# Operands of the input projection and of stick-breaking attention kept in DRAM in two parts, and half of the weights' rests formed in PSUM

## The chip, the cores and the metric

The kernel runs on one core of one Trainium2 chip. The metric is the device time of one execution in microseconds. PE is TensorE, DVE VectorE, ACT ScalarE, POOL GpSimd; SP is the queue that issues most DMAs.

## The reference, cut to what matters

The reference is one layer of a decoder trunk in float32: 2048 tokens, width 1024. One projection feeds four groups of heads; their outputs are normed, projected and followed by an MLP.

```python
h = rms_norm(x, norm1_w[l])
cols = split_cols(h @ w_in[l], IN_SIZES)
...
s_q, s_k, s_v = cols[14:17]
...
y_d = stick_breaking_mixer(s_q.reshape(B, S, SB_HEADS, HEAD_DIM), s_k.reshape(B, S, SB_HEADS, HEAD_DIM),
                           s_v.reshape(B, S, SB_HEADS, HEAD_DIM))
```

The group of heads that the change touches is the last one, with 4 heads of 64 columns:

```python
def stick_breaking_mixer(q, k, v):
...
        z = jnp.einsum('bqhd,bkhd->bhqk', q_blk, k).astype(f32) * scale
        strict = kpos[None, :] < (t0 + jnp.arange(Q_BLOCK))[:, None]
        log_1m = jnp.where(strict, jax.nn.log_sigmoid(-z), 0.0)
        rem = lax.cumsum(log_1m, axis=3, reverse=True) - log_1m
        a = jnp.where(strict, jnp.exp(jax.nn.log_sigmoid(z) + rem), 0.0)
        return jnp.einsum('bhqk,bkhd->bqhd', a.astype(v.dtype), v)
```

## The kernel before, in words

Products of two float32 matrices are made of float32r products: an operand is split in a high part (a copy rounded to float32r) and a low part, the rest (operand minus high part), and three products high·high, high·low and low·high are summed in PSUM. `split_s` (L212) does the split: ACT copies the high part, another engine, mostly DVE, subtracts.

The program has three phases: `front`, the attention phase (`attention.main`) and `tail` (output projection and MLP). The change lies in `front` and in `stick`, which `front` runs in its last part.

**The projection.** The transposed, normed input is held for half of the tokens at a time (`hth`, `htl`). The weight columns are cut in ten chunks ("nq", "m", "nk", "sv" with tokens on the partitions, 0 to 5 with columns on the partitions; 2540 columns in all). For each chunk and each half of the tokens an object of the class `Weights` (L367) loads eight row blocks of the weights (`wraw`, L378) and splits each (`wh`, `wl`, L386, scaled by the norm's weight). So every block of the weights is loaded and split twice, once per half. `ch_mm` and `tok_mm` make the products, 24 per output tile. `channel` (L614) and `sb_v` (L608) store the columns of the stick-breaking q, k and v to DRAM (`sbqd`, `sbkd`, `sbvd`), unsplit. In the second half the chunks "nk", 3, 4 and 5 are held back: they are the filling work of `others()`.

**Stick-breaking attention.** `stick` (L1196) goes through 4 heads and 4 blocks of 512 queries each (16 units); `ahead` loads a unit's q, k and v as `srq`, `srk`, `srv` and splits them (`qq` and `sql`, `kk`, `svp`). For each unit and each of its key blocks `weights` makes, per 128 queries, the logits (PE to `pmm`), two sigmoids on ACT (`bt`, `sg`), a scan on DVE that multiplies up the products from the right (`ce`, L1256) and a product on POOL (`sg`, L1258). One step later `values` transposes the weights 128 keys at a time (PE, L1297, to `ptr`), splits the 128x512 result (`ah` by ACT, `al` by DVE, L1301), and `product` multiplies both parts with the values (`svp`, to `pacc`). There are 160 such splits: 112 of 512 columns and 16 each of 384, 256 and 128.

**What sets the order.** The last loop of `front` pairs the steps of `stick` with steps of `others()` at a fixed rate (150 filling steps on 388 steps of `stick`), each filling step being placed behind the last product issued. Beyond that the framework's scheduler orders the instructions of each engine. The first part of the attention phase's preparation (`nx.early()`) also runs as filling work.

## Time and profile before

| | |
|---|---|
| median of 3 runs | 3097.89 us (3091.86 to 3104.19) |
| the profiled execution | 3101.34 us, of which the span of its instructions is 3099.6 us |
| mean granted clock of TensorE | 0.970 |
| projection, first half of the tokens | 0 to about 333 us |
| projection, second half, without the chunks held back | about 333 to 509 us |
| `stick` with its filling work | about 509 to 905 us |
| attention phase, then the tail | from 905 us to the end |

The profile gives busy time per engine; a view by stretches gives the busy time in each stage, the granted clock of PE (1 is 2.4 GHz, one half is 1.2 GHz) and the share of the DMA engines. The time before an engine's instruction in which it stood idle is put down to whatever released that instruction last.

### The profile page before, as it was taken

The numbers are of one execution on the slowest core, as the hardware profiler recorded it, in microseconds if no ns is written. First come the engines' busy times: TensorE is split into PE (matmuls) and PEld (weight loads), VectorE is DVE, ScalarE is ACT, GpSimd is POOL, SyncE is SP. The second block draws the span as 40 slices with busy tenths as digits, with TensorE's granted clock in tenths as the row PEclk, the third lists the DMA queues.
The fourth block names the chain that finished last, engine by engine and source line by source line (L and its number), as shares of the span: only waits on it lengthen the run. The fifth ranks groups of instructions, "written<-read, shape, count | busy, mean of one in ns | idle before, by whom it ended". The sixth has DMA issues, their size and how long they took to land. (4 is left out here: it accounts for less than half of the span.)

```text
span 3099.6 us, 43934 instructions
## 1 busy us (share of the span) xinstructions
PE 2921.3 (94%) x14123; PEld 2327.5 (75%) x14123; DVE 2301.5 (74%) x4894; ACT 1693.7 (55%) x3440; POOL 1353.4 (44%) x1311
## 2 busy tenths in 40 slices
PE   7999999899888999998989989999999999989999
PEld 7868888677755666666768778787888778877887
DVE  7844478998877686777668777657444599999999
ACT  5622455777775778786765444456555533324331
POOL 1300012444655666765622257735222244364434
PEclk9999999899988999999999999999999999999999
DMA  6343434211320110010034468936333544365432
GB/s 162 100 113 86 128 97 110 61 53 45 84 84 23 28 33 22 29 42 15 9 114 143 170 212 299 314 107 203 110 109 109 211 163 156 122 206 172 150 131 73
DMA packets 283977, 356.49 MB, mean 115 GB/s; under 512 B 74207, under 2 KB 185483, under 8 KB 283491
## 3 DMA queue, kind: packets, MB, share of 16 engines
q1 hardware_dynamic: 251859, 310.03, 32.1%
q10 hardware_dynamic: 31344, 41.82, 3.6%
q0 software_dynamic: 544, 1.84, 0.2%
q8 instruction: 112, 1.84, 0.2%
q14 instruction: 118, 0.97, 0.1%
HBM read 248.04 MB, written 105.59 MB: 114 GB/s over the span
## 5 line engine op out<-in xcount | busy, mean ns | idle before, releaser
L931 POOL TENSOR_TENSOR pw<-pf,ph 128x512 fp32r<-128x512 f32 (+2 forms) x264 | 325.9, 1243 | 170.0 <-ACT pf L930 120.8
L138 PE MATMUL ptr<-form,big 128*128 128x512 f32 x1152 | 280.4, 392 | 7.8 <-ACT ft L1857 4.2
L138 PE MATMUL pmm<-form,big 128*128 128x512 f32 x1152 | 278.5, 391 | 0.9 <-ACT big L216 0.9
L925 ACT ACTIVATE ph<-pmm 128x512 fp32r<-128x512 f32 (+2 forms) x366 | 210.7, 576 | 102.0 <-PE pmm L138 67.7
L138 PEld LDWEIGHTS ptr<-form,big 128*128 128x128 f32 x1152 | 216.3, 188 | 56.9 <-ACT ft L1857 5.1
L138 PEld LDWEIGHTS pmm<-form,big 128*128 128x128 f32 x1152 | 216.1, 188 | 48.1 <-ACT big L216 1.3
L1258 POOL TENSOR_TENSOR sg<-sg,ce 128x512 f32<-128x512 f32 (+3 forms) x160 | 161.3, 1009 | 178.6 <-DVE ce L1256 130.8
L138 PE MATMUL pmm<-big 128*128 128x512 f32 (+5 forms) x816 | 217.2, 394 | 4.7 <-DVE accp L2054 2.4
L216 ACT ACTIVATE big<-raw 128x1024 fp32r<-128x1024 f32 (+2 forms) x116 | 100.9, 883 | 183.7 <-PE ptr L138 106.4
L138 PE MATMUL pmm<-big,big 128*128 128x512 f32 (+5 forms) x672 | 178.1, 392 | 12.2 <-DVE accp L2054 10.0
L138 PE MATMUL pmm<-big,ar 128*128 128x512 f32 x736 | 185.1, 401 | 1.9 <-DVE ar L217 1.9
L138 PEld LDWEIGHTS pmm<-big 128*128 128x128 f32 (+2 forms) x816 | 154.4, 193 | 40.8 <-ACT op L216 5.2
L217 DVE TENSOR_TENSOR big<-hr,big 128x512 fp32r<-128x512 f32 (+1 forms) x125 | 136.8, 1096 | 60.2 <-ACT big L216 60.1
L138 PE MATMUL ptr<-big 128*128 128x512 f32 (+3 forms) x639 | 174.8, 396 | 4.5 <-DVE mx L1153 2.1
L217 DVE TENSOR_TENSOR big<-yr,big 128x512 fp32r<-128x512 f32 (+1 forms) x125 | 130.7, 1048 | 53.9 <-ACT big L216 53.5
L138 PEld LDWEIGHTS pmm<-big,ar 128*128 128x128 f32 x736 | 138.2, 191 | 32.4 <-DVE ar L217 2.4
L2054 DVE TENSOR_TENSOR accp<-accp,ptr 128x512 f32<-128x512 f32 x224 | 151.8, 678 | 13.0 <-PE ptr L138 12.6
L2054 DVE TENSOR_TENSOR accp<-accp,pmm 128x512 f32<-128x512 f32 x224 | 151.7, 677 | 9.7 <-PE pmm L138 9.7
L138 PEld LDWEIGHTS pmm<-big,big 128*128 128x128 f32 (+2 forms) x672 | 125.0, 189 | 43.2 <-DVE accp L2054 10.9
L138 PE MATMUL ptr<-big,big 128*128 128x512 f32 (+3 forms) x512 | 144.4, 402 | 8.3 <-DVE accp L2054 3.7
L930 ACT ACTIVATE pf<-pmm 128x512 f32<-128x512 f32 (+2 forms) x264 | 152.2, 577 | 0.0
L138 PEld LDWEIGHTS ptr<-big 128*128 128x128 f32 (+1 forms) x639 | 121.7, 191 | 36.0 <-DVE mx L1153 3.8
(504 smaller groups left out, 8384.2 us busy)
## 6 DMA issues: line engine op xcount, KB each, us to landing
ud<-ft ACTq DMA_DIRECT2D x124, 256.0 KB, 2.0
xt<-x SPq DMA_DIRECT2D x32, 512.0 KB, 3.5
yr<-ffn_w SPq DMA_DIRECT2D x16, 1024.0 KB, 5.1
hr<-ffn_w SPq DMA_DIRECT2D x16, 1024.0 KB, 5.9
rawb<-ffn_w SPq DMA_DIRECT2D x28, 512.0 KB, 6.8
wsd<-rawb SPq DMA_DIRECT2D x28, 512.0 KB
rawb<-ud SPq DMA_DIRECT2D x28, 512.0 KB, 4.3
raw<-wsd SPq DMA_DIRECT2D x28, 512.0 KB, 3.5
```

What stands on the lines that cost most here:

```text
L138: anchor[0] = pe.matmul(o, l, r, start=start, stop=stop)
L216: act.activation(hi, src, AF.Copy)
L217: (eng or dve).tensor_tensor(lo, src, hi.bitcast(F32), ALU.subtract)
L925: act.activation(ph[:, 0:n], pl[:, 0:n], AF.Exp)
L930: act.activation(pf[:, 0:n], pl[:, 0:n], AF.Exp)
L931: sub.tensor_tensor(pw[:, 0:n], pf[:, 0:n], ph[:, 0:n].bitcast(F32), ALU.subtract)
L1258: pool.tensor_tensor(sg[:, o:512], sg[:, o:512], ce[:, o + 1:513], ALU.mult)
L2054: dve.tensor_tensor(acc[p][:, t], acc[p][:, t], pt, ALU.add)
```

## The change

It does three things.

1. The first half stores each split block of weights (both parts, one tile `whl`) to DRAM arrays `kept`, three blocks behind the split; the second half loads the two parts from there and splits nothing.
2. The stick-breaking q, k and v are split where they leave PSUM, and both parts are stored; `ahead` only loads the parts to where they are used.
3. In `values`, for every second 128 keys, the transposed weights stay in PSUM as an open sum. ACT copies the high part, PE adds the product of that part with minus the identity, so the low part is left in PSUM, and ACT copies that. The other splits stay.

```diff
+            def store_weights(left):
+                while len(stores) > left:
+                    o, w = stores.pop(0)
+                    sync.dma_start(o, w)
...
                 def load(self, k):
                     while len(self.ws) <= k:
                         n = self.n
                         c = len(self.ws)
+                        whl = wp.tile([P, 2, CW], F32R, name="whl", tag="whl", bufs=NWT)
+                        wh, wl = whl[:, 0], whl[:, 1]
+                        self.ws.append((wh, wl))
+                        if not self.first:
+                            sync.dma_start(whl[:, :, :n].bitcast(F32), self.kept[c])
+                            continue
...
-                        wh = wp.tile([P, CW], F32R, name="wh", tag="wh", bufs=12)
-                        wl = wp.tile([P, CW], F32R, name="wl", tag="wl", bufs=12)
                         split_s(raw[:, :n], wh[:, :n], wl[:, :n], n1w[:, c:c + 1],
                                 heng=pool if self.raw is not None and c % 2 else None)
-                        self.ws.append((wh, wl))
+                        stores.append((self.kept[c], whl[:, :, :n].bitcast(F32)))
+                        store_weights(3)
...
+            def sb_v(i, pt):
+                vt = op.tile([P, H, 2, HD], F32R, name="vhl", tag="cout")
+                split_s(pt[:, 0:256].rearrange("p (h d) -> p h d", h=H), vt[:, :, 0], vt[:, :, 1])
+                sync.dma_start(sbvd[i * P:(i + 1) * P].rearrange("p h c -> p (h c)"),
+                               vt.rearrange("p h s d -> p (h s d)").bitcast(F32))
...
-                    if kind in ("q", "k", "kv"):
+                    if kind in ("q", "k"):
+                        hl = [op.tile([P, 512], F32R, name="chl%d" % n, tag="cout") for n in range(2)]
+                        split_s(pt, *hl)
+                        for o, t in zip(sbqd if kind == "q" else sbkd, hl):
+                            sync.dma_start(o[ct * P:(ct + 1) * P, t0:t0 + 512], t.bitcast(F32))
...
+        minus = kp.tile([P, P], F32R, name="minus")
+        act.activation(minus, ident, AF.Copy, scale=-1.0)
...
-                sync.dma_start(rk[g * 64:(g + 1) * 64, :], sbkd[hs, tsl])
-                sync.dma_start(rq[g * 64:(g + 1) * 64, :], sbqd[hs, tsl])
-            sync.dma_start(rv, sbvd[tsl, hs].rearrange("(i p) d -> p i d", p=P))
-            yield
-            act.activation(kk, rk, AF.Copy)
-            dve.tensor_tensor(kk[64:128], rk[64:128], kk[64:128].bitcast(F32), ALU.subtract)
-            yield
-            act.activation(qq, rq, AF.Copy)
-            dve.tensor_tensor(ql[0:64], rq[0:64], qq[0:64].bitcast(F32), ALU.subtract)
-            yield
-            split_s(rv, vp[:, :, 0:64], vp[:, :, 64:128])
-            yield
+                sync.dma_start(kk[g * 64:(g + 1) * 64, :].bitcast(F32), sbkd[g][hs, tsl])
+                sync.dma_start(qq[g * 64:(g + 1) * 64, :].bitcast(F32), sbqd[0][hs, tsl])
+            sync.dma_start(ql[0:64].bitcast(F32), sbqd[1][hs, tsl])
+            sync.dma_start(vp.bitcast(F32), sbvd[tsl, h].rearrange("(i p) d -> p i d", p=P))
+            for _ in range(4):
+                yield
...
-                    pe.transpose(pt[:, t * P:(t + 1) * P], sgs[t][:, o + jj * P:o + (jj + 1) * P], ident)
+                    pe.matmul(pt[:, t * P:(t + 1) * P], sgs[t][:, o + jj * P:o + (jj + 1) * P], ident,
+                              start=t == f, stop=False, is_transpose=True, skip_group_check=True)
...
-                split_s(pt[:, f * P:], ah[:, f * P:], al[:, f * P:])
+                if jj % 2:
+
+                    act.activation(ah[:, f * P:], pt[:, f * P:], AF.Copy)
+                    if flight:
+                        product()
+                    pe.matmul(pt[:, f * P:], minus, ah[:, f * P:], start=False, stop=True, skip_group_check=True)
+                    act.activation(al[:, f * P:], pt[:, f * P:], AF.Copy)
+                else:
+                    split_s(pt[:, f * P:], ah[:, f * P:], al[:, f * P:])
```

How the scheduler then orders the work is shown at three places. The first is DVE about halfway through `stick`, at the end of a unit's last key block and the start of the next: `ce` are scans, `al` the low parts of transposed weights. Before:

```order
L1256 SCALAR_TENSOR_TENSOR ce_9967<-bt_9966,pmm_9968 128x512
L217 TENSOR_TENSOR al_9871<-ptr_9865,ah_9870 128x512
L217 TENSOR_TENSOR al_9908<-ptr_9902,ah_9907 128x512
L217 TENSOR_TENSOR al_9934<-ptr_9928,ah_9933 128x512
L1256 SCALAR_TENSOR_TENSOR ce_9990<-bt_9989,ce_9878,pmm_9991 128x512
L1256 SCALAR_TENSOR_TENSOR ce_10022<-bt_10021,ce_9915,pmm_10023 128x512
L1256 SCALAR_TENSOR_TENSOR ce_10047<-bt_10046,ce_9941,pmm_10048 128x512
L217 TENSOR_TENSOR al_9957<-ptr_9951,ah_9956 128x512
```

The same place now:

```order
L1275 SCALAR_TENSOR_TENSOR ce_9673<-bt_9672,pmm_9674 128x512
L218 TENSOR_TENSOR al_9577<-ptr_9571,ah_9576 128x512
L218 TENSOR_TENSOR al_9639<-ptr_9633,ah_9638 128x512
L1275 SCALAR_TENSOR_TENSOR ce_9696<-bt_9695,ce_9584,pmm_9697 128x512
L1275 SCALAR_TENSOR_TENSOR ce_9727<-bt_9726,ce_9620,pmm_9728 128x512
L1275 SCALAR_TENSOR_TENSOR ce_9752<-bt_9751,ce_9646,pmm_9753 128x512
L218 TENSOR_TENSOR al_9689<-ptr_9683,ah_9688 128x512
```

Of four subtractions between the scans two are left; the scans stand as they did.

The second place is the same stretch on PE. `cp,sg` are the transposes, `minus` the new product, `pacc1` the products with the values, `kk,qq` and `kk,sql` the logits. Before, eight transposes are followed by logits and by the products of earlier parts:

```order
L1297 MATMUL ptr_9928<-cp_63,sg_9764 128x128
L1297 MATMUL ptr_9928<-cp_63,sg_9793 128x128
L1297 MATMUL ptr_9928<-cp_63,sg_9823 128x128
L1297 MATMUL ptr_9928<-cp_63,sg_9850 128x128
L138 MATMUL pmm_10023<-kk_9529,qq_9661 128x512
L138 MATMUL pmm_10023<-kk_9529,sql0_7012 128x512
L138 MATMUL pmm_10048<-kk_9529,qq_9661 128x512
L138 MATMUL pmm_10048<-kk_9529,sql0_7012 128x512
L138 MATMUL pacc1_9790<-ah_9870,svp_9053 128x512
L138 MATMUL pacc1_9790<-al_9871,svp_9053 128x512
```

Now:

```order
L1316 MATMUL ptr_9606<-cp_63,sg_9530 128x128
L1316 MATMUL ptr_9606<-cp_63,sg_9556 128x128
L1325 MATMUL ptr_9542<-ah_9544,minus_6840 128x128
L139 MATMUL pacc1_9495<-ah_9544,svp_9249 128x256
L139 MATMUL pmm_9753<-kk_9247,qq_9368 128x512
L139 MATMUL pmm_9753<-kk_9247,sql0_6842 128x512
L1325 MATMUL ptr_9606<-ah_9611,minus_6840 128x512
L139 MATMUL pacc1_9495<-al_9545,svp_9249 128x256
```

And ACT's copies around the same product, now:

```order
L217 ACTIVATE ah_9576<-ptr_9571 128x512
L1322 ACTIVATE ah_9611<-ptr_9606 128x512
L1326 ACTIVATE al_9545<-ptr_9542 128x128
L1272 ACTIVATE bt_9751<-pmm_9753 128x512
L1326 ACTIVATE al_9612<-ptr_9606 128x512
```

On PE four other products stand between the last transpose into this bank (`ptr_9606`) and the product with minus the identity; over the 80 of them the count goes from 2 to 28 (two of the 80 have under 4, half have 14 or more). On ACT the copy of the low part stands mostly 3 to 8 instructions behind that of the high part. Behind the last transpose of `stick` PE's order is the same, row for row, as before.

The third place is SP at the start of the program. Before:

```order
L422 DMA xt<-x 128x1024 x3
L464 DMA gq<-mla_q_norm 96x1
L465 DMA gq<-mla_k_norm 96x1
L564 DMA ngn<-nsa_q_norm 64x1
L565 DMA ngn<-nsa_k_norm 64x1
L564 DMA ngn<-nsa_q_norm 64x1
```

Now:

```order
L436 DMA xt<-x 128x1024 x3
L487 DMA gq<-mla_q_norm 96x1
L488 DMA gq<-mla_k_norm 96x1
L587 DMA ngn<-nsa_q_norm 64x1
L588 DMA ngn<-nsa_k_norm 64x1
L370 DMA kept_nq<-whl 256x1x256 x5
```

Five stores of split weights now stand ahead of the fifth load of x. Over the whole program SP issues 1244 DMAs where it issued 1172: 120 loads of `w_in` fewer, 80 stores to and 80 loads from `kept` more, 16 more stores of q and k, and 16 more loads in `ahead`.

## Rows read from the trace of the kernel before

**Rows 1.** The page: busy time, share of the span and instructions of each engine.

```profile
PE 2921.3 (94%) x14123; PEld 2327.5 (75%) x14123; DVE 2301.5 (74%) x4894; ACT 1693.7 (55%) x3440; POOL 1353.4 (44%) x1311
```

**Rows 2.** Busy time by stretches: engines, granted clock, DMA share, GB/s.

```profile
0.00:333.00 333.00, 307.20 (x1730) 262.11 (x1731) 200.32 (x799) 144.75 (x334) 61.31 (x91) 0.97 0.44 114
333.00:509.00 176.00, 172.31 (x1067) 153.59 (x1066) 110.02 (x432) 87.91 (x232) 23.90 (x73) 1.00 0.42 113
509.00:905.00 396.00, 345.07 (x1881) 276.29 (x1880) 364.93 (x657) 287.93 (x653) 196.45 (x373) 0.93 0.26 70
1100.00:1300.00 200.00, 187.73 (x925) 134.19 (x926) 149.02 (x417) 153.13 (x350) 133.09 (x131) 0.96 0.10 29
2200.00:2600.00 400.00, 392.55 (x1696) 318.88 (x1695) 255.93 (x330) 189.88 (x276) 128.93 (x73) 0.99 0.42 146
```

**Rows 3.** Waits of PE, 509 to 905 us: total us, times, longest us.

```profile
PE pmm L138 <- DVE ce L1256: 24.4, 28, 4.7
PE pacc L138 <- DVE al L217: 7.0, 11, 1.6
PE pmm L138 <- DVE rky L199: 4.0, 3, 3.0
PE pmm L138 <- DVE rkt L198: 3.5, 3, 2.9
```

**Rows 4.** Groups of DVE, 509 to 905 us: busy us, mean ns, idle before.

```profile
L1256 DVE TENSOR_TENSOR_SCAN ce<-bt,ce,pmm 128x512 f32<-128x512 f32 x96 | 119.5, 1266 | 4.8 <-ACT sg L1254 4.2 <-POOL ce L1251 0.3 <-issue 0.3
L217 DVE TENSOR_TENSOR al<-ptr,ah 128x512 fp32r<-128x512 f32 (+3 forms) x160 | 92.1, 595 | 3.9 <-ACT ah L216 3.5
L1256 DVE TENSOR_TENSOR_SCAN ce<-bt,pmm 128x128 f32<-128x128 f32 (+1 forms) x64 | 50.4, 806 | 2.9 <-ACT sg L1254 0.8 <-issue 0.7 <-POOL al L1303 0.5
L223 DVE SCALAR_TENSOR_TENSOR wl<-wraw,n1w,wh 128x256 fp32r<-128x256 f32 (+2 forms) x28 | 18.3, 668 | 1.0 <-ACT wh L220 0.9
L1224 DVE TENSOR_TENSOR kk<-srk,kk 64x512 fp32r<-64x512 f32 x16 | 13.0, 815 | 1.0 <-ACT kk L1223 0.4
L1227 DVE TENSOR_TENSOR sql<-srq,qq 64x512 fp32r<-64x512 f32 x16 | 12.1, 755 | 0.5 <-PE ptr L1297 0.4
L217 DVE TENSOR_TENSOR svp<-srv,svp 128x256 fp32r<-128x256 f32 x16 | 8.8, 549 | 3.4 <-ACT svp L216 3.3
```

**Rows 5.** Groups of ACT, 509 to 905 us.

```profile
L216 ACT ACTIVATE ah<-ptr 128x512 fp32r<-128x512 f32 (+3 forms) x160 | 84.7, 548 | 48.3 <-PE ptr L1297 38.6 <-DVE ce L1256 3.7 <-issue 2.6
...
L220 ACT ACTIVATE wh<-wraw,n1w 128x256 fp32r<-128x256 f32 (+2 forms) x28 | 13.1, 502 | 8.3 <-DMA wraw<-w_in 7.8 <-PE pacc L138 0.3
L1223 ACT ACTIVATE kk<-srk 128x512 fp32r<-128x512 f32 x16 | 10.4, 647 | 1.9 <-DMA srk<-sbkd 1.9
L1226 ACT ACTIVATE qq<-srq 128x512 fp32r<-128x512 f32 x16 | 10.3, 646 | 1.9 <-PE pmm L138 1.8
...
L216 ACT ACTIVATE svp<-srv 128x256 fp32r<-128x256 f32 x16 | 7.0, 434 | 0.5 <-DMA srv<-sbvd 0.5
```

**Rows 6.** Timeline of PE in `stick`: start us, us, engine, line, operation.

```profile
706.40 0.39 PE L138 MATMUL pacc<-hth,wh 128*128 128x512 f32 x1
706.63 0.40 PE L138 MATMUL pacc<-htl,wh 128*128 128x512 f32 x1
```

**Rows 7.** DMA issues, 509 to 905 us: count, KB each, median us to landing.

```profile
srk<-sbkd SPq DMA_DIRECT2D x32, 128.0 KB, 2.8
...
wraw<-w_in SPq DMA_DIRECT2D x40, 64.0 KB, 2.1
```

**Rows 8.** Timeline of SP at the start: loads of norm weights, then the fifth x load.

```profile
8.30 0.47 SPq L564 DMA_DIRECT2D ngn<-nsa_q_norm  x1
...
15.48 0.35 SPq L422 DMA_DIRECT2D xt<-x  x1
```

**Rows 9.** Waits of PE, 333 to 509 us, the longest in total.

```profile
PE pmm L138 <- ACT m L230: 1.0, 1, 1.0
```

More of the change, by code (lines that the diff above doesn't have):

```diff
@@ L244, in _build @@
     mvd = dram.tile([S, H * HD], F32, name="mvd")
-    sbqd = dram.tile([2 * P, S], F32, name="sbqd")
-    sbkd = dram.tile([2 * P, S], F32, name="sbkd")
-    sbvd = dram.tile([S, H * HD], F32, name="sbvd")
+    sbqd = [dram.tile([2 * P, S], F32, name="sbqd%d" % n) for n in range(2)]
+    sbkd = [dram.tile([2 * P, S], F32, name="sbkd%d" % n) for n in range(2)]
+    sbvd = dram.tile([S, H, 2 * HD], F32, name="sbvd")
     yd = dram.tile([S, D], F32, name="yd")
@@ L446, in x_tile @@
                     split_s(pt.rearrange("p (c t) -> p c t", c=4), hth[o], htl[o])
-            early = Weights([(768, 256)], oq.tile([P, KC, 256], F32, name="wearly", tag="kc2", bufs=1))
+            CH = [[("kv", 0), ("q", 0)], [("q", 1), ("k", 0)], [("k", 1), ("c", 0)], [("u", 0), ("b", 0)],
+                  [("c", 1), ("u", 1)], [("b", 1)]]
+            cols = {"kv": 1024, "q": 1772, "k": 2028, "c": 256, "u": 512, "b": 0}
+            pieces = {"m": [(1420, 352)], "nq": [(768, 256)], "nk": [(1152, 268)], "sv": [(2284, 256)]}
+            for n, sl in enumerate(CH):
+                pieces[n] = [(cols[kd] + ct * P, P) for (kd, ct) in sl]
+            kept = {c: dram.tile([KC, P, 2, sum(p[1] for p in v)], F32, name="kept_%s" % c)
+                    for c, v in pieces.items()}
+            early = Weights(pieces["nq"], kept["nq"], True, oq.tile([P, KC, 256], F32, name="wearly", tag="kc2", bufs=1))
             x_load(0)
@@ L814, in tok_chunk @@
                     pt = yield from tok_mm(ii, w)
-                    m = op.tile([P, CW], F32, name="m", tag="m", bufs=3)
-                    evac(m[:, :n], pt[:, :n])
-                    run_side()
-                    live.append(use(i, m))
+                    if use is sb_v:
+                        sb_v(i, pt)
+                        run_side()
+                    else:
+                        m = op.tile([P, CW], F32, name="m", tag="m", bufs=3)
+                        evac(m[:, :n], pt[:, :n])
+                        run_side()
+                        live.append(use(i, m))
                     if now == "next" and ii >= 1:
@@ L856, in front @@
                     side.append(compress())
-            early = Weights(pieces["nk"])
+            early = Weights(pieces["nk"], kept["nk"], False)
             early.load(KC - 1)
@@ L1208, in ahead @@
             hs = slice(h * HD, (h + 1) * HD)
-            rk = wp.tile([P, 512], F32, name="srk", tag="srk", bufs=1)
-            rq = wp.tile([P, 512], F32, name="srq", tag="srq", bufs=1)
-            rv = wp.tile([P, 4, HD], F32, name="srv", tag="srv", bufs=1)
             kk = wp.tile([P, 512], F32R, name="kk", tag="kk", bufs=5)
```

26 lines of the change are left out of this document (10 added, 16 removed).

## Prediction

> **What bounds the kernel now.** I read the page's first part, then the busy time by stretches, then the waits and groups of the one stretch that stands out. On the page PE is busy for 94% of the span, no other engine for more than 74% [rows 1]. So time can only be had where PE stands, and the stretches show where [rows 2]. In the tail PE is busy for 392.55 of 400 us, in the second half of the projection for 172.31 of 176. In the stretch of `stick`, 509 to 905 us, it is busy for 345.07 of 396: 50.9 us idle, at a mean granted clock of 0.93, so that part of the busy time ran at the lower of the two levels, 1.2 GHz instead of 2.4. In that stretch the busiest engine is not PE but DVE, 364.93 of 396 us, 92% [rows 2]. And PE's waits there name it: 24.4 us for the scan `ce`, which still held a bank of logits, 7.0 us for `al`, the rest in small sums behind other work of DVE [rows 3]. This stage is bound by DVE, with PE close behind. The attention phase (1100 to 1300 us) serves as yardstick: PE 94%, DVE 75%, ACT 77%, POOL 67%, clock 0.96. So much does PE reach in this kernel when no other engine is full.
>
> **The change in `stick`, DVE.** All groups are in [rows 4]. Every second `al` goes: 48 of 512 columns, 16 of 384 and 16 of 128, taken as half of the group's 92.1 us, 46. The subtractions in `ahead` go: 13.0 + 12.1 + 8.8 = 33.9. The low parts of the weights of the chunks held back go, 18.3. Together 98 us: DVE falls from 365 to 267 us. The scans (119.5 + 50.4) stay.
>
> **ACT.** The high parts of the same operands go: 13.1 + 10.4 + 10.3 + 7.0 = 40.8 us. Eighty copies of low parts come; at the mean of `ah`, 548 ns, that is 43.8 [rows 5]. ACT stays at about 291 us. POOL keeps its 196.
>
> **PE.** Eighty products with minus the identity come. No row shows one, but it is a float32r product with 128 rows like those around it: two starts of 512 columns lie 0.23 us apart [rows 6]. The 48 full ones cost 11.0 us, the others in proportion to their columns 2.8 and 0.9: 14.7 us. The transposes stay as many.
>
> **The sum.** DVE at 267 us and ACT at 291 leave no engine full, so I let the stage run as the attention phase does. PE's busy time of 345.1 us was taken at a clock of 0.93; at 0.96 I put it at 345.1 x 0.93 / 0.96 = 334.3, plus 14.7 makes 349. At the yardstick's busy share, 187.73 / 200 = 0.939, the stage takes 371.8 us instead of 396: 24 us less. At that length DVE is busy 72%, ACT 78%, POOL 53% of it, close to the yardstick, which is why I choose it between the two ends: without the return of the clock (345.1 + 14.7) / 0.939 = 383, 13 us less; with PE at the tail's share (392.55 / 400 = 0.981) 349 / 0.981 = 356, 40 us less.
>
> **What may stand in the new places.** PE could stand at the product with minus the identity until ACT has copied the high part. Nothing of it: if the products ordered in between cover it, and half of the 80 have 14 or more between, 14 x 0.23 = 3 us against 0.55 for the copy. All of it: 80 x 0.548 = 43.8 us. I take the low end, a few us, which is in the yardstick's 6% of idle time. The operands in `ahead` now land where PE reads them, one landing of 2.8 us [rows 7] instead of landing plus split. If each of the 16 units showed it, 16 x 2.8 = 45 us; none if the load goes out during the unit before, as it is issued at that unit's first step. PE waits for no load now [rows 3], and I take 0.
>
> **The projection.** In its first half the 80 stores add 20.8 MB (2540 columns x 1024 rows x 8 bytes). The DMA share is 0.44 at 114 GB/s there [rows 2]; 62 GB/s more, in proportion, makes 0.68, so bandwidth is left. At the start five stores stand ahead of the fifth load of x; at 0.47 us an issue [rows 8] that is 2.4 us, between 0 and 2.4 for PE, and I take 1, since the stores also wait for their splits. The split of q, k and v at PSUM adds one subtraction for each of 32 tiles to a stage where DVE is busy 200 of 333 and 110 of 176 us; it is covered there. In the second half 48 blocks are loaded in two parts and not split: a landing takes 2.1 us for 64 KB and 2.8 for 128 KB [rows 7], the new loads move 256 KB or so, and six of the eight blocks of a chunk can be loaded ahead (14 buffers). Taking the 2.8 us, at most 10 x 2.8 = 28 us if every chunk showed one, and at best the 3.7 us of PE's idle time there [rows 2], whose longest wait is 1.0 us [rows 9]. I take 1 us less. The two cancel. Behind `stick` PE and SP have the same order, and I take no change.
>
> **The number.** The sum is made against the profiled execution, 3101.3 us (span 3099.6): 3077. The median of the runs shown is 3.4 us lower, 3097.9, and minus 24 us gives **3074 us**, 0.8% less. What a measurement of this kernel can tell from no change is about 0.5%, 15.5 us: faster begins below 3082.4, slower above 3113.4.
>
> **Rivals.**
>
> *All waits go.* DVE drops so far that PE fills up as in the tail, 40 us less as worked out above: 3058. For it: most of the idle time of PE is DVE's [rows 3], and DVE loses 27% of its work. Against: ACT and POOL are chained to PE here as in the attention phase, and the yardstick has never reached it. The Trainium skill (Perfetto Trace Analysis, Identifying the Most-Contended Engine) says that the busy share of matmuls is a bad measure of PE's room and that of weight loads a good one; by it this stage has more room, since weight loads are busy 70% here against 80% in the tail [rows 2], and the sum would be this rival's. The trace bears it out only in part: the attention phase has weight loads at 67% and no engine full, and yet does not go faster.
>
> *The wait changes its name.* DVE's waits go, but PE now waits for ACT, which does three passes for each full split of half of the units and has the sigmoids in the same queue; the clock does not come back. Then the gain is 0 to 13 us, about 3090. For it: ACT already waits 38.6 us for transposes before `ah` [rows 5], so its order is not the order in which PE delivers. Against: it is only 73% busy, and the copies stand several instructions apart.
>
> *PE stands at the new product (slower).* The scheduler's order holds only if ACT is as early as it supposes. If each of the 80 products waits for one whole copy, 43.8 us of idle time come on top of the forecast: 24 less becomes 20 more, 3118. It decides at a mean stand of 24 / 80 = 0.30 us; above (24 + 15.5) / 80 = 0.49 us the kernel is slower by more than can be missed. For it: PE takes its products in order, and what is behind one that waits, logits and transposes, waits too, and with it the scans. Against: the distance on PE, above.
>
> *The change does nothing.* If the bound were PE's own work in this stretch, DVE's relief would be worth nothing and the 14.7 us would be added: 3113. Against: 50.9 us of idle time.
>
> **Chances.** Forecast (roughly 3066 to 3082) 0.42, all waits go 0.18, the wait changes its name 0.25, with the case of no use in it, PE stands 0.15, most of it above 3113. So faster by over 0.5% 0.60, within 0.5% 0.26, slower 0.14. The range goes from 3050, a little under the first rival, to 3106, which leaves out the upper part of the last two: about 2 in 10.
>
> **What would show it.** Right: the stretch from the first scan to the last is 15 to 35 us shorter; DVE is busy about 267 us in it, ACT about 290; PE's waits for `ce` fall under 10 us; the granted clock rises to about 0.96; the new products start 0.23 us apart from their neighbours, and PE's waits for `ah` and for the landing of `kk`, `qq` and `svp` stay under 10 us together. Wrong: PE waits for `ah` at L1325 for 25 us or more, or for loads of `whl` in the second half of the projection, or the stage ends where it did with ACT named as the releaser.

## The result, and the profile after

The changed kernel takes 3121.89 us (median of 6 runs, 3112.78 to 3124.92); the kernel before, run beside it, 3098.06 us (6 runs). The ratio is 1.0065, with a 95% interval of 1.005 to 1.0081: 24 us **slower**, by a little more than the 0.5% set as the bound, where 24 us faster was predicted. The range (3050 to 3106) does not hold it.

The profiled execution took 3124.2 us, its span 3122.4. Its page begins with the busy times, answering to [rows 1]: DVE is 82 us less busy, PE 15 us more.

```profile
PE 2935.9 (94%) x14203; PEld 2335.4 (75%) x14203; DVE 2219.5 (71%) x4702; ACT 1674.8 (54%) x3409; POOL 1344.1 (43%) x1311
```

To place the 22.8 us between the two spans, both were cut at the same instructions, within 1 us: the last transpose of x (325.6 us before, 340.9 after), the first and the last transpose of weights in `stick`, and the start of the last stage of the tail. The views by stretches (length, then busy time of PE, PEld, DVE, ACT, POOL, granted clock, DMA share, GB/s) are, before:

```profile
0.00:325.00 325.00, 299.50 (x1694) 255.93 (x1695) 199.03 (x797) 143.19 (x332) 61.31 (x91) 0.97 0.44 115
325.00:525.80 200.80, 195.26 (x1218) 173.56 (x1217) 127.12 (x521) 100.45 (x265) 25.98 (x78) 1.00 0.42 113
525.80:903.00 377.20, 328.05 (x1761) 261.52 (x1759) 347.81 (x571) 276.35 (x622) 192.67 (x361) 0.93 0.25 67
903.00:2452.00 1549.00, 1479.24 (x6800) 1135.16 (x6799) 1031.17 (x2333) 946.12 (x1966) 782.09 (x656) 0.97 0.33 112
2452.00:3099.60 647.60, 619.24 (x2659) 501.31 (x2657) 596.32 (x677) 227.63 (x258) 291.34 (x125) 0.98 0.45 150
```

and after:

```profile
0.00:340.00 340.00, 301.90 (x1692) 256.93 (x1693) 197.32 (x793) 140.90 (x327) 60.60 (x91) 0.96 0.63 184
340.00:544.00 204.00, 198.36 (x1225) 175.90 (x1223) 111.97 (x486) 82.59 (x227) 26.82 (x79) 0.99 0.54 163
544.30:921.60 377.30, 331.54 (x1833) 262.70 (x1831) 277.91 (x417) 277.46 (x631) 184.82 (x360) 0.97 0.30 84
921.60:2468.00 1546.40, 1480.84 (x6802) 1136.34 (x6800) 1022.64 (x2333) 946.63 (x1968) 782.58 (x656) 0.97 0.34 112
2468.00:3122.00 654.00, 622.98 (x2658) 503.21 (x2656) 609.36 (x676) 226.95 (x257) 289.24 (x125) 0.98 0.44 150
```

- **First half of the projection: +15 us.** PE does the same work (299.5 and 301.9 us busy) in 15 us more, with the DMA share up from 0.44 to 0.63.
- **Second half: +3 us.**
- **`stick`: 0.** DVE is 70 us less busy, the clock is back from 0.93 to 0.97, and the stage is as long as it was. All that was hoped for lies here.
- Behind it: 3 us less in the attention phase and first part of the tail, 7 us more in the last stage. The instructions there did not change. In the profiles of this study that stage takes from 647 to 655 us, with these two kernels at the ends; what moves it is open.

In `stick` (544 to 922 us) the waits have changed their names. Columns: engine, tile and line, what ended the wait; total us, times, longest. PE first, answering to [rows 3], then DVE:

```profile
PE pmm L139 <- DVE ce L1275: 31.7, 40, 6.1
PE pmm L139 <- DVE rky L200: 4.3, 3, 2.1
PE ptr L1316 <- DVE al L218: 2.7, 4, 1.5
PE ptr L1325 <- ACT ah L1322: 1.5, 2, 1.0
...
DVE ce L1275 <- ACT sg L1273: 38.3, 33, 3.7
DVE al L218 <- ACT ah L217: 13.0, 15, 1.9
```

PE still stands for the scan `ce`, longer than before (31.7 us against 24.4), though DVE is now busy for only 74% of the stage. The scan itself is late: DVE waits 38.3 us for `sg`, the second sigmoid on ACT. In the kernel before that was:

```profile
DVE ce L1256 <- ACT sg L1254: 5.0, 11, 0.7
```

How much of this reaches PE directly is less than it looks. Of PE's 31.7 us, 7.6 end with a scan before which DVE had itself stood idle (4.3 of 24.4 in the kernel before; both worked out from the trace). The rest end with scans that started right behind other work of DVE.

The new product (L1325) is hardly waited at: 1.5 us. ACT's groups (count, busy us, mean ns, idle before and its releasers), answering to [rows 5]:

```profile
L1272 ACT ACTIVATE bt<-pmm 128x512 f32<-128x512 f32 (+3 forms) x155 | 86.4, 570 | 18.2 <-PE pmm L139 17.4
L1273 ACT ACTIVATE sg<-pmm 128x512 f32<-128x512 f32 (+3 forms) x155 | 82.5, 559 | 9.7 <-PE ptr L1316 9.7
L217 ACT ACTIVATE ah<-ptr 128x512 fp32r<-128x512 f32 x80 | 46.5, 582 | 13.8 <-PE ptr L1316 13.2 <-PE pacc L139 0.4
L1326 ACT ACTIVATE al<-ptr 128x512 fp32r<-128x512 f32 (+1 forms) x79 | 42.6, 539 | 9.1 <-PE ptr L1325 9.1
L1322 ACT ACTIVATE ah<-ptr 128x512 fp32r<-128x512 f32 (+1 forms) x79 | 41.5, 525 | 36.5 <-PE ptr L1316 36.4
```

ACT has its two sigmoids per bank of logits and its copies in one queue, and it stands for 36.4 us before the new copies `ah` until PE has made their transposes. Where such a copy is ordered between the two sigmoids of one bank, the second sigmoid waits too, and with it the scan. The timeline of ACT shows one such place (start us, us, line, operation, idle before):

```profile
676.46 0.91 ACT L1272 ACTIVATE bt<-pmm 128x512 f32<-128x512 f32 x2
681.59 0.28 ACT L1322 ACTIVATE ah<-ptr 128x128 fp32r<-128x128 f32 x1 [4.22 <-PE ptr L1316]
681.77 0.59 ACT L1273 ACTIVATE sg<-pmm 128x512 f32<-128x512 f32 x1
682.27 0.60 ACT L217 ACTIVATE ah<-ptr 128x512 fp32r<-128x512 f32 x1
682.77 0.38 ACT L1272 ACTIVATE bt<-pmm 128x256 f32<-128x256 f32 x1
683.03 0.60 ACT L1322 ACTIVATE ah<-ptr 128x512 fp32r<-128x512 f32 x1
683.52 0.28 ACT L1326 ACTIVATE al<-ptr 128x128 fp32r<-128x128 f32 x1
684.51 0.49 ACT L1272 ACTIVATE bt<-pmm 128x384 f32<-128x384 f32 x1 [0.71 <-PE pmm L139]
684.90 0.59 ACT L1326 ACTIVATE al<-ptr 128x512 fp32r<-128x512 f32 x1
687.29 0.60 ACT L217 ACTIVATE ah<-ptr 128x512 fp32r<-128x512 f32 x1 [1.80 <-PE ptr L1316]
687.78 0.94 ACT L1273 ACTIVATE sg<-pmm 128x128 f32<-128x128 f32 x3
```

The second of the two `bt` at 676.46 began at 676.94. Its `sg` is among the three at 687.78, 11 us later, with six copies in between. PE had other products in this stretch and stood for scans for only 1.0 us between 676.5 and 690, so the place shows how a sigmoid comes late, not what that costs. Counted over the stage, 45 of the 160 pairs of sigmoids had a copy `ah` or `al` between them before, and 76 have one now; three or more copies stood between 4 pairs before, and between 31 now.

### The profile page after: what moved, and what is told of

It reads as the page before. It is cut to its first block, busy times and chain, and to the rows that moved or that the text cites. A ratio compares the mean times of both kernels' runs of the same rounds, so it can differ in the third digit from the quotient of the medians.

```text
span 3122.4 us, 43803 instructions
## 1 busy us (share of the span) xinstructions
PE 2935.9 (94%) x14203; PEld 2335.4 (75%) x14203; DVE 2219.5 (71%) x4702; ACT 1674.8 (54%) x3409; POOL 1344.1 (43%) x1311
## 5 line engine op out<-in xcount | busy, mean ns | idle before, releaser
L139 PE MATMUL pmm<-whl,hth 128*128 128x256 f32 (+2 forms) x896 | 189.7, 303 | 5.0 <-ACT hth L217 3.8
L139 PE MATMUL pmm<-hth,whl 128*128 128x512 f32 x544 | 176.4, 402 | 0.3 <-ACT hth L217 0.3
L139 PEld LDWEIGHTS pmm<-whl,hth 128*128 128x128 f32 x896 | 147.4, 193 | 11.2 <-ACT hth L217 4.9
```

The lines of the kernel that those rows point to most:

```text
L139: anchor[0] = pe.matmul(o, l, r, start=start, stop=stop)
```

## The experiments

Three theories were open. **PE's work**: the 80 new products cost what they are long, since PE's idle time is not where they stand. **The order on ACT**: the new copies come between the two sigmoids of a bank of logits, which is held meanwhile, so the scan and PE's next logits are late. **The ring**: there are three banks of logits, and how long one is held sets the stage by itself. For the first half of the projection: the bytes of the stores, or their place in SP's queue.

The table gathers what the runs gave. "Total" is the median, "beside" that of the kernel before run beside it. The last four columns are from the profiled execution: the stage from the first to the last transpose of `stick`, PE's idle time in it, the mean time from the first logits written to a bank to the end of its scan ("held", worked out from the trace), and the last transpose of x.

| run | total | beside | ratio (95%) | stage | PE idle | held | x done |
|---|---|---|---|---|---|---|---|
| before | 3098.06 | | | 377.3 | 49 | 5.79 | 325.6 |
| the change (parts 1, 2, 3) | 3121.89 | 3098.06 | 1.0065 (1.005 to 1.0081) | 377.2 | 46 | 6.10 | 340.9 |
| e1: parts 1, 2 | 3094.49 | 3103.45 | 0.9972 (0.9959 to 0.9986) | 351.0 | 35 | 5.31 | 341.2 |
| e2: part 3 | 3119.57 | 3103.45 | 1.0056 (1.0036 to 1.0077) | 401.2 | 59 | 6.44 | 325.2 |
| e3: parts 2, 3 | 3123.38 | 3103.45 | 1.007 (1.0052 to 1.0089) | 389.7 | 47 | 6.27 | 327.6 |
| e4: scan without PSUM | 3157.61 | 3103.45 | 1.0175 (1.016 to 1.019) | 411.2 | 61 | 6.13 | 338.0 |
| e5: stores on ACT's queue | 3129.25 | 3105.53 | one run | 378.5 | 41 | 6.07 | 342.7 |
| e6: e1 with 32 stores of 80 | 3096.08 | 3105.53 | 0.9966 (0.9953 to 0.9978) | 353.2 | 36 | 5.23 | 331.7 |
| e7: every fourth logits in a bank for transposes | 3185.96 | 3105.53 | one run | 465.9 | 96 | | 326.0 |
| e9: before, one sigmoid | 3095.72 | 3105.53 | 0.9967 (0.9955 to 0.9979) | 366.3 | 42 | 5.22 | 323.6 |
| e10: e6, one sigmoid | 3083.78 | 3102.26 | 0.9941 (0.9926 to 0.9956) | 335.5 | 27 | 4.48 | 330.6 |
| e11: the change, one sigmoid | 3093.63 | 3102.26 | 0.9977 (0.9962 to 0.9993) | 352.3 | 30 | 4.91 | 339.4 |
| e12: low part copied by DVE | 3119.08 | 3102.26 | 1.0054 (1.0038 to 1.007) | 377.7 | 44 | 5.96 | 338.7 |
| e13: e1 with 80 idle products | 3104.52 | 3101.11 | 1.0014 (1.0004 to 1.0024) | 360.6 | 35 | 5.29 | 341.5 |

For e4 "held" ends with the second sigmoid, which is there the last to read the bank. Each of the last four columns comes from one execution, and a difference of a few us in them says little: the first half of the projection is the same in four of the kernels (before, e2, e7, e9) and ends there between 323.6 and 326.0 us.

### e1: the change without part 3

```diff
-                    pe.matmul(pt[:, t * P:(t + 1) * P], sgs[t][:, o + jj * P:o + (jj + 1) * P], ident,
-                              start=t == f, stop=False, is_transpose=True, skip_group_check=True)
+                    pe.transpose(pt[:, t * P:(t + 1) * P], sgs[t][:, o + jj * P:o + (jj + 1) * P], ident)
...
-                if jj % 2:
+                if False:
```

> This is the changed kernel with every rest of the transposed weights taken by DVE again (parts 1 and 2 of the change alone). Theory RING: the stage of stick, first to last transpose, took 377.3 us before and 377.2 after because three PSUM banks hold the logits until two passes of ACT and the scan of DVE are done (mean hold 5.8 us before, 6.1 after; 160 x 6.1 / 3 = 325 us). Taking the 80 copies out of ACT's queue brings the scan earlier, since it waits for ACT now: the hold falls under 5.8 us and the stage to 355 to 372 us, the kernel to 3100 to 3117. Theory DVE-BOUND (the prediction's): DVE gets 46 us back, so the stage grows to 385 to 400 us and the kernel to 3130 to 3145. Theory PE-STANDS: the products with minus the identity cost PE what was gained, 15 us of work and 5 of waits: stage 357, kernel 3102.

The stage falls to 351.0 us, 26 less than with part 3, and the kernel is 0.3% faster than before in spite of the first half. All three theories missed the length (355 to 372, 385 to 400 and 357 us), and DVE-BOUND is out: DVE got its subtractions back, and the stage became shorter. In `stick`:

```profile
548.00:899.00 351.00, 315.95 (x1752) 253.98 (x1751) 310.27 (x492) 248.04 (x552) 185.16 (x360) 0.95 0.32 89
```

Parts 1 and 2 take 37.5 us off DVE and 28 off ACT, and the stage gives back 26. Part 3 takes another 32 us off DVE, and the stage grows by 26.

### e2: part 3 alone, on the kernel before

```diff
...
+                if jj % 2:
+                    act.activation(ah[:, f * P:], pt[:, f * P:], AF.Copy)
...
+                    pe.matmul(pt[:, f * P:], minus, ah[:, f * P:], start=False, stop=True, skip_group_check=True)
+                    act.activation(al[:, f * P:], pt[:, f * P:], AF.Copy)
+                else:
+                    split_s(pt[:, f * P:], ah[:, f * P:], al[:, f * P:])
```

> This is the kernel before with the product with minus the identity alone (part 3). The first half of the projection must take what it took before (last transpose of x at 325 us), whatever the theory on stick. RING: ACT now carries the splits of operands (41 us) and the 80 copies (43), and the scan waits for ACT: hold 6 us or more, stage 377 to 395 us, kernel 3098 to 3116. DVE-BOUND: DVE loses 46 us of 365, stage 360 to 370, kernel 3082 to 3092.

```profile
526.10:927.30 401.20, 342.17 (x1839) 271.20 (x1838) 316.02 (x491) 306.90 (x702) 196.14 (x361) 0.94 0.25 63
```

The stage takes 401.2 us, 24 more than before: part 3 costs about the same, whether parts 1 and 2 are there or not, and the first half of the projection is untouched (325.2). Neither range holds the stage (377 to 395, 360 to 370). DVE, the busiest engine of the kernel before, has 32 us less to do here and ACT 31 more, and the stage is longer: taking work off DVE was not worth anything in this form.

### e3: the change without part 1

```diff
-                        if not self.first:
-                            sync.dma_start(whl[:, :, :n].bitcast(F32), self.kept[c])
-                            continue
...
-                        stores.append((self.kept[c], whl[:, :, :n].bitcast(F32)))
-                        store_weights(3)
...
```

The weights are loaded and split as in the kernel before.

> This is the changed kernel without part 1: weights are loaded and split in both halves, nothing is stored to or loaded from kept. The first half of the projection took 15 us more after the change (last transpose of x at 340.8 us against 325.5). Theory STORES: SP's queue and the DMA engines carry 20.8 MB of stores, and what PE waits for in the first half (the tables' round trips through DRAM, weights) lands later: without them the last transpose of x is back at 325 to 328 us and the kernel at 3106 to 3110, if stick does not move. Theory TILES: the split q and k take both tiles of the tag cout at once and hold them for two stores each, so ACT and DVE stand for cout (40 us in the waits) and PE behind them: the last transpose of x stays at 335 to 341 us. In stick 24 weight splits (18 us DVE, 13 us ACT) come back; RING expects 0 to 8 us more there, DVE-BOUND 18 more.

Part 1 costs 13.3 us in the first half (327.6 against 340.9) and gains 12.5 in `stick` (389.7 against 377.2): nothing on balance. The total agrees, 3123.38 against 3121.89. For the first half STORES holds (325 to 328 us) and TILES falls (335 to 341). The 12.5 us lie between RING's 0 to 8 and DVE-BOUND's 18.

### e4: the scan reads no PSUM

The scan's second operand is not used by its operation (it is bypassed), and in the kernel it is the bank of logits. Here it is `bt`, in SBUF; nothing is left out.

```diff
-                dve.tensor_tensor_scan(ce[:, o:512][:, ::-1], bt[:, o:512][:, ::-1], pz[:, 0:w], carry,
+                dve.tensor_tensor_scan(ce[:, o:512][:, ::-1], bt[:, o:512][:, ::-1], bt[:, o:512][:, ::-1], carry,
```

> This is the changed kernel with one operand of the scan changed: its second data operand, which the scan does not use (the second operation is a bypass), is the sigmoid in SBUF instead of the logits in PSUM, so the bank of logits comes free after ACT's second pass. RING: the hold loses the wait for DVE and the scan (median 0.4 us from the second sigmoid to the scan and 1.1 for the scan, and the wait of the scan for the second sigmoid): stage 345 to 365 us instead of 377, PE's waits for ce (31.7 us) go, kernel 3090 to 3110. DVE-BOUND or PE-STANDS: the bank is not what counts: stage within 5 us of 377, kernel 3117 to 3127. Against RING in any case: a scan that reads SBUF twice may be slower, or slow POOL's products.

The scan is freed, 120 of 160 now start before the second sigmoid of their bank has ended, and the kernel is 1.75% slower. The bank is held no shorter (6.13 us): the second sigmoid ends 4.27 us after the start of the first, where it was 2.95. Neither range for the stage holds (345 to 365, within 5 of 377). And the scan itself became slower, together with POOL's work. DVE's and POOL's groups in the change:

```profile
L1275 DVE TENSOR_TENSOR_SCAN ce<-bt,ce,pmm 128x512 f32<-128x512 f32 x96 | 119.2, 1268 | 25.9 <-ACT sg L1273 17.4 <-issue 8.0
...
L1270 POOL COPY ce<-ce 128x1 f32<-128x1 f32 x96 | 19.5, 203 | 0.0
```

and in e4:

```profile
L1275 DVE TENSOR_TENSOR_SCAN ce<-bt,ce 128x512 f32<-128x512 f32 x96 | 152.4, 1612 | 35.5 <-ACT bt L1272 28.7 <-issue 3.7 <-POOL al L1331 2.3
...
L1270 POOL COPY ce<-ce 128x1 f32<-128x1 f32 x96 | 56.7, 593 | 30.9 <-DVE ce L1275 24.2 <-DVE rkt L199 2.9 <-DVE rky L196 2.0
```

So the run changed two things at once and does not test the ring. It does say that a bank held as long as in the change can go with a stage 34 us longer.

### e5: the stores of part 1 on ACT's queue

```diff
-                    sync.dma_start(o, w)
+                    act.dma_start(o, w)
```

> This is the changed kernel with the 80 stores to kept issued from ACT's queue instead of SP's; the same bytes move. Taking part 1 away gave the first half 13 us back (last transpose of x 340.9 us with it, 327.6 without). SP-QUEUE: the stores cost because loads and the tables' round trips stand behind them on SP's queue: with the stores elsewhere the last transpose of x is at 326 to 332 us. TRAFFIC: they cost because 20.8 MB more go through the same DMA engines, and every other transfer of the stage takes longer to land: it stays at 336 to 343 us.

The last transpose of x comes at 342.7 us, not earlier than with SP's queue (340.9). So far as one run tells, the place in SP's queue is not what costs. TRAFFIC has the right range, but what in the transfers costs is not shown: in the first 340 us ACT waits for loads of weights for 48.1 us in the change (24.5 in the first 325 us before), and for only 24.1 here, with no gain for PE.

### e6: parts 1 and 2 with fewer stores

On top of e1's edit, only the chunks held back ("nk", 3, 4 and 5) are stored and loaded in two parts: 32 of the 80 blocks.

```diff
-                        if not self.first:
+                        if not self.first and self.late:
...
-                        stores.append((self.kept[c], whl[:, :, :n].bitcast(F32)))
-                        store_weights(3)
+                        if self.late:
+                            stores.append((self.kept[c], whl[:, :, :n].bitcast(F32)))
+                            store_weights(3)
```

> No product with minus the identity, and only the chunks nk, 3, 4 and 5, whose second half lies beside stick, are stored and loaded split: 32 stores instead of 80; the other chunks are split in both halves. Under both theories on the stores their cost in the first half falls to 28/80 to 32/80 of 13 us, 4 to 6 us (last transpose of x at 330 to 333 us), while stick keeps what e1_no_minus had (351 us, hold 5.3 us). So 8 us less than e1_no_minus: 3083 to 3090. If the first half's loss comes from the early chunks alone, 326 us and 3080; if the second half's splits cost PE anything, up to 3095.

x is done at 331.7 us. In proportion to the number of stores, 32/80 of e3's 13.3 us, it would be 333. With nearly all of the stage's gain kept (353.2), the kernel is 0.34% faster than before; against e1 (0.28%) the intervals overlap, so the 8 us less than e1 that were expected are not shown.

### e7: a fourth bank for the logits

```diff
-                pz = pmm()
+                pz = ptr() if j == 3 else pmm()
```

> This is the kernel before in which every fourth block of logits takes its PSUM bank from the ring of ptr (three banks, otherwise for transposes and table work) instead of pmm's. RING: the ring of logits gets relief where it binds; 120 blocks share three banks, 120 x 5.8 / 3 = 232 us instead of 309, and the ring of transposes, held 2 to 4 us for each of 160 blocks, takes 40 more: stage 345 to 370 us instead of 377 (kernel 3070 to 3095). DVE-BOUND: DVE has the same 365 us of work, so the stage stays at 372 to 382.

A miss, in one run. The ring of the transposes was robbed, and PE stood there too, and longer than before at the logits (38.7 us against 24.4); its waits in the stage are

```profile
PE pmm L138 <- DVE ce L1256: 38.7, 48, 2.2
PE ptr L1297 <- DVE ce L1256: 27.8, 24, 2.9
```

Three banks serve the logits, three the transposes and two the sums, so a longer ring was not tried without shortening another; the ring by itself stays untested.

### e9: one sigmoid in the kernel before

The second sigmoid (`sg`) goes; the weight is formed by POOL as the difference of two neighbours of the scan.

```diff
-                act.activation(sg[:, o:512], pz[:, 0:w], AF.Sigmoid, scale=0.125)
...
-                pool.tensor_tensor(sg[:, o:512], sg[:, o:512], ce[:, o + 1:513], ALU.mult)
+                pool.tensor_tensor(sg[:, o:512], ce[:, o + 1:513], ce[:, o:512], ALU.subtract)
```

> This is the kernel before without the second sigmoid: the weight is the difference of two neighbours of the scan (1 - b times the product is the product less the next one), so POOL subtracts where it multiplied, and ACT makes one pass over a bank of logits instead of two. RING: the hold loses one pass of 0.55 us and what stands between the passes (from the first sigmoid's start to the second's end 1.9 us, of which one pass remains): hold 4.3 to 5.0 us, stage 335 to 362 us, kernel 3058 to 3085. DVE-BOUND: DVE's 365 us stay, stage 370 to 380, kernel 3090 to 3102.

ACT is 62 us less busy and the stage gains only 11. DVE, at 339.7 of 366.3 us, no longer waits before its scans:

```profile
L1255 DVE TENSOR_TENSOR_SCAN ce<-bt,ce,pmm 128x512 f32<-128x512 f32 x96 | 119.8, 1264 | 0.4 <-issue 0.2
```

Neither range holds the stage (335 to 362, 370 to 380); it is nearer to DVE-BOUND's. So ACT's busy time did not bound the kernel before. That DVE did, as the prediction says, fits: it runs here without waiting at its scans, and is busy for 93% of the stage.

### e10: e6 with one sigmoid

The diff is that of e6 and of e9 together.

> Kernel after without the product with minus identity, with the stores of the two parts for the chunks nk, 3, 4 and 5 alone, and without the second sigmoid: POOL forms the weight as the difference of two neighbours of the scan, which is the same quantity. BANKS (what bounds stick is how long a bank of logits is held, and the copies and sigmoids of ACT lengthen that): the two gains come in different places, DVE relieved (353 us of stick alone) and ACT's second pass gone (366 alone, where DVE was the bound), so they add up and more: the stage takes 320 to 340 us, the bank is held under 5 us, the kernel 3060 to 3085 us, ratio 0.987 to 0.994. PE (with DVE relieved PE is the bound at about 350 us): the stage stays at 345 to 355, the kernel at 3090 to 3098.

The two gains add up: 335.5 us, 3083.78 us in total, 0.59% faster than before (0.9926 to 0.9956). It is the fastest version of the study. Of the 17.7 us by which the stage is shorter than e6's, a part lies in its later start: from the last transpose of x to the first of `stick` it takes 212.1 us here and 205.6 in e6. By the totals e10 is 0.25% faster than e6, 8 us. That it would add up was the expectation BANKS; PE's limit is not yet reached at 350 us. PE is now busy for 92% of the stage and DVE for 89%:

```profile
542.60:878.00 335.40, 308.06 (x1746) 248.90 (x1745) 297.61 (x475) 186.80 (x396) 174.63 (x355) 0.96 0.34 92
```

### e11: the change with one sigmoid

The change in full, with e9's edit.

> Kernel after, all three parts, without the second sigmoid: POOL forms the weight as the difference of two neighbours of the scan, which is the same quantity. SIGMOIDS (the product with minus identity costs 26 us because ACT's new copies come between the two sigmoids of a bank that is held meanwhile): with one sigmoid nothing stands in between, the stage falls from 377 to 340 to 355 us, the bank is held about 5 us, the kernel 3088 to 3100 us. CHAIN (it costs because copy, product and copy again follow one another while a bank of transposed weights is held and PE waits in order): the second sigmoid is beside it, the stage falls by no more than the 11 us that it gave the kernel before, to 365 to 377 us, the kernel at 3108 to 3120.

```profile
543.60:896.00 352.40, 322.58 (x1831) 261.16 (x1830) 266.52 (x414) 217.57 (x476) 177.06 (x360) 0.97 0.34 89
```

SIGMOIDS holds in its size; its reason is not shown. The same edit that gave the kernel before 11 us gives the changed one 25, 16 of them from PE's idle time (46 to 30). By the totals the edit is worth 0.33% (10 us) in the kernel before, 0.25% (8 us) from e6 to e10, where DVE is relieved and part 3 is missing, and 0.88% (27 us) in the change, each to within about 0.2%. So part 3 and the second sigmoid cost more together than each by itself. That the copies between the two sigmoids are the reason was only argued, and the edit also takes 60 us off ACT. And part 3 is not free even so. Against e10, which has no part 3 (and fewer stores, worth 2 us of the stage between e1 and e6), PE is 14.5 us longer busy and 2.5 us longer idle, and the stage is 17 us longer.

### e12: the low part copied by DVE

```diff
-                    act.activation(al[:, f * P:], pt[:, f * P:], AF.Copy)
+                    dve.tensor_copy(al[:, f * P:], pt[:, f * P:])
```

> Kernel after, but the low part that the product with minus identity leaves in PSUM is copied by DVE and not by ACT. ACT (the cost of part 3 lies in ACT's 80 added copies, PE's 80 products cost next to nothing): ACT falls from 286 to about 245 us of the stage, DVE rises from 293 to about 335, the bank is held 5.3 to 5.6 us, the stage takes 350 to 362 us, the kernel 3094 to 3108. PE (the cost lies in the products themselves and in the order that they force on PE): the stage stays at 370 to 380 us, the kernel at 3115 to 3125.

```profile
542.40:920.10 377.70, 333.63 (x1831) 266.64 (x1830) 312.74 (x495) 249.72 (x552) 185.73 (x360) 0.95 0.31 84
```

The theory that ACT's 80 added copies are the cost falls. ACT is as little busy as in e1 (249.7 and 248.0), DVE as much (312.7 and 310.3), and the stage is 27 us longer than e1's. What is left as the difference is the product on PE, which adds 17.7 us of busy time, and the chain of copy, product and copy, with the order that the scheduler makes of it: copies stand between 66 of the 160 pairs of sigmoids, 43 in e1.

Late sigmoids do not account for this length. DVE's waits for the second sigmoid and PE's waits for the scan are, in e1 and then here:

```profile
DVE ce L1273 <- ACT sg L1271: 11.7, 18, 2.0
PE pmm L139 <- DVE ce L1273: 27.9, 34, 5.6
```

```profile
DVE ce L1275 <- ACT sg L1273: 13.4, 13, 2.9
PE pmm L139 <- DVE ce L1275: 30.2, 37, 2.9
```

Both are nearly as in e1, and the stage is as long as the change's, in which DVE waits 38.3 us. PE stands 9 us longer than in e1, in several small waits.

### e13: 80 products that nothing waits for

e1, with one product of minus identity and zeros ahead of every second group of transposes, which overwrite it.

```diff
+                if jj % 2:
+                    pe.matmul(pt[:, f * P:], minus, blank[:, f * P:], start=True, stop=True, skip_group_check=True)
```

> Parts 1 and 2 alone (351.0 us of stick, kernel 3094.5), plus 80 products of minus identity with a tile of zeros, one ahead of each second group of transposes, into the bank that the transposes then overwrite. They add nothing to the result, no copy and no wait for a copy. With part 3 the stage was 26 us longer, of which 15 to 18 us were PE's own busy time and 9 to 11 us further standing of PE. WORK (a product more on PE is paid in full, since what PE stands for elsewhere in the stage gives no room): the stage takes 363 to 371 us, PE busy 14 to 18 us more, its idle time stays at about 35 us, the kernel 3106 to 3116. COVER (PE's idle time covers them, and what part 3 cost is the chain copy, product, copy): the stage stays at 349 to 357 us, PE's idle time falls to 20 us or so, the kernel at 3092 to 3100.

```profile
545.70:906.30 360.60, 325.62 (x1833) 263.50 (x1832) 307.93 (x496) 249.68 (x552) 184.06 (x360) 0.95 0.33 87
```

PE is busy 9.7 us more and the stage is 9.6 us longer; PE's idle time is 35 us in both. WORK's size was too large (14 to 18), its mechanism is borne out: idle time of PE gave these products no cover at all. By the totals (1.0014 against 0.9972) they cost 13 us. So of the 26 us of part 3, about 10 are the products themselves, and the other 16 or so come with the copies and with the order that the scheduler makes of copy, product and copy. The split is rough: in the change PE is busy 15.6 us more than in e1 and idle 10.7 us more. And by which path the 16 us come is open: the late sigmoids stand in the change and not in e12.

## Why the prediction was wrong, point by point

**What bounds the stage: right in the main.** ACT's busy time did not (e9), and parts 1 and 2 alone, which take 37.5 us off DVE and 28 off ACT, brought 26 us in `stick` (e1), where the prediction had 24 for the whole change. No run relieved DVE alone, and 32 us moved from DVE to ACT (e2) brought nothing, so the bound was not DVE's busy time by itself.

**"DVE falls from 365 to 267 us": mostly right.** Between the first and the last transpose it fell by 70 us, not 98. The groups named did go (by their durations 92 us within these bounds), but durations of DVE overlap (386 us of them make 348 us of busy time in the kernel before), and the busy time falls by less than their sum.

**ACT and PE: right as terms.** ACT's busy time is as it was (276.4 and 277.5). PE's 80 products start 0.23 us after their neighbour, as taken from [rows 6]; PE, in the change:

```profile
700.48 0.40 PE L139 MATMUL pmm<-kk,qq 128*128 128x512 f32 x1
700.72 0.40 PE L1325 MATMUL ptr<-ah,minus 128*128 128x512 f32 x1
700.95 0.39 PE L139 MATMUL pacc<-ah,svp 128*128 128x512 f32 x1
```

The 14.7 us compare with 14.1 to 17.7 us of added busy time in the four pairs of kernels without and with part 3 (before and e2, e1 and the change, e1 and e12, e10 and e11). The clock came back, 0.97 against the 0.96 predicted.

**The step that failed: "At the yardstick's busy share, 187.73 / 200 = 0.939, the stage takes 371.8 us".** PE's share stayed where it was, 331.54 / 377.3 = 0.879 against 328.05 / 377.2 = 0.870. The attention phase was a yardstick for engines that are not full; it says nothing of what PE waits for in `stick`. Two things are wrong in it. The relief was taken as one sum of 98 us, though it stopped counting once DVE was no longer the bound: after parts 1 and 2, part 3's own 32 us off DVE bought nothing (e12 has them back on DVE and 28 us less on ACT, and its stage is as long as the change's, 377.7 against 377.3). And the 14.7 us of PE were put under a share that rises, though in this stage a product more is paid in full (e13). The 16 us or so that came with the copies and their order were not in the sum.

**"PE could stand at the product with minus the identity ... I take the low end": right, and beside the point.** PE waits 1.5 us there. The rival that PE stands at the new product gave nearly the right time, 3118, by the wrong mechanism. Of the signs of being wrong that the prediction names, another came: the stage ends where it did, with ACT named, here as the one that releases DVE's scans (38.3 us). How much this delays PE is not settled (7.6 us of its standing directly, and e12 is as long without it).

**The rival "The wait changes its name"** has the waits of the change: DVE waits for ACT, and PE for the scan. It expected the clock not to come back, and it did. It foresaw 0 to 13 us of gain; the stage gave 0, and it did not see that part 3 alone loses 24 to 27. What it wanted was to be read further: the order on ACT, shown ahead of the prediction, has the new copies on both sides of a `bt`. Counting copies between the sigmoids of one bank needed no run.

**The rule on weight loads**, from the Trainium skill (Perfetto Trace Analysis, Identifying the Most-Contended Engine), foresaw more room on PE. After the change weight loads are busy 262.70 / 377.3 = 70%, as before. That room was not to be had: with 80 products more e13 got longer by their whole length. One sigmoid less brought weight loads to 74% (e10).

**"The projection ... PE 0 to 2.4, and I take 1": wrong by 14 us.** The DMA share was foreseen well (0.68; it is 0.63 at 184 GB/s), but "so bandwidth is left" does not follow. The cost is smaller with fewer stores (e6) and is not that of SP's queue (e5, one run). It is spread over many small waits of PE. The largest that grew, in the first 340 us, is for one table, first before and then after:

```profile
PE ptr L138 <- DMA tb<-extd: 6.8, 3, 4.5
```

```profile
PE ptr L139 <- DMA tb<-extd: 11.1, 4, 5.3
```

Which resource of the transfers is short was not found out. In the second half the 1 us less that was taken came out as 3 us more.

**The sum.** Parts 1 and 2 bring -26 us in `stick`, part 3 brings +26, the first half +15 (13 of them from part 1, by e3), the second half +3; the rest, +4 on balance, lies in stages where nothing was changed and is not explained. Without part 3 and with fewer stores, the change would have been a gain (e6), though of less than half of the 24 us forecast (0.34%, 10.5 us).

**What stays open.** By which path part 3's copies and their order cost about 16 us, and whether the time that a bank of logits is held sets the stage by itself. Over the runs the time held goes along with the stage (4.48 us and 335 in e10, 6.44 and 401 in e2), but it can as well follow from it: e13 lengthens the stage at the same 5.3 us as e1, and e7, meant to decide it, disturbed another ring.

## What to carry to other kernels

When a change takes work off the bound engine in several parts, find at which part the bound moves on; later parts may be worth nothing, as part 3 was here, while what they add to other engines may be paid in full, as its products were. Where an in-order engine serves two chains (here the sigmoids that feed the scan, and the copies that feed the products), read its order before its busy share: a copy that waits for another engine holds up the other chain behind it, as at 676 to 688 us above; what that costs must still be tried. And a DMA share of 0.6 is not proof that stores beside a loading stage are free.

## What the runs showed of the hardware that was not expected

- A scan of 128x512 takes 1268 ns with its unused operand in PSUM and 1612 ns with that operand in SBUF. Meanwhile POOL's copies of 128x1 go from 203 to 593 ns, and its products `sg` from a mean of 978 to 1100. So in this kernel the operand in PSUM goes with a faster scan and with faster work of POOL (e4); why is not shown.
- The scan never starts before the second sigmoid of the same bank has ended: in all 160 cases, in the kernel before and in the change, by 0.03 us at the least, although its values don't depend on it. With the operand in SBUF, 120 of 160 do. The Trainium skill (PSUM — Partial Sum Buffer, PSUM bank collisions raise a hardware error) says that two engines must not access one bank at once and that a scheduler orders such instructions, reads among them; the trace agrees with such an order, and does not show who makes it. In this kernel the readers of one bank therefore add up in time, and each of them waits for what stands ahead of the other in its queue.
